# Layer 1's gate product: every second block on two float16 parts, and another order at attention's two ends

## The chip, the cores and the metric

The kernel runs on one NeuronCore of a Trainium2 chip. The metric is device time in microseconds (us), the median of several executions. TensorE (PE) multiplies, VectorE (DVE) and ScalarE (ACT) work on tiles elementwise, GpSimd (POOL) helps with some subtractions, and SyncE (SP) issues most transfers. Each engine takes its instructions strictly in the order in which they were written for it; engines wait for each other through semaphores.

## What is computed

The reference is a two-layer transformer block stack for 256 tokens of width 2048, with 256 context tokens. Layer 0 is a Fourier mixer, layer 1 attention with a sink. The change concerns layer 1:

```python
def _attention_branch(h, hc, w_in, sink, rows, cols, need_ctx):
    q, k, v, z = jnp.split(h @ w_in, [D_BRANCH, D_BRANCH + kvw, D_BRANCH + 2 * kvw], axis=-1)
    ...
    y = jnp.moveaxis(o, 0, 1).reshape(b, n, D_BRANCH) * jax.nn.silu(z)
```

Here `h` is 256 x 2048, `q` and `z` are 256 x 4096 each, and `y` is multiplied by the output weights afterwards (`x + gate * (y @ w_out[1])`). `z` is the gate product of the title.

## The kernel before

Every large product is made of three matmuls on parts (`mm3`: high x high, high x low, low x high), so that two short parts stand for one float32 number. The parts come in two kinds. `half_split` makes two float32r parts of half a loaded weight tile: a copy on ACT (`split`, L66) and a subtraction on DVE (L67). `split16` makes two float16 parts: the tile times a scale on ACT (L137) and the rest on DVE (L138). float16 needs the scale, since its range is small; the scale is a power of two from the sum of squares of the weights.

Layer 1 begins with the keys and values of all 512 tokens, on float16 parts of the activations (`hz`, 16 tiles) in a pool of their own. The activations `hx1` (16 tiles, float32r parts) then serve the queries and the gate.

Then comes the attention loop. The weights are taken in *units*, each half of a 1 MB tile `raw` (three buffers): a q unit has 12 matmuls of 512 columns, a z unit 24 matmuls of 256 columns, an o unit (first output columns) 12 of 512. `units()` writes their order out: q of head 0, and then per group of four blocks the 8 q units of the next head and the 2 x 4 z units of the four blocks of 128 channels; 14 o units at the end. `prep` makes the parts of a unit one unit ahead; their pool `ws` has six buffers, two to a unit.

The blocks b = 0..31 (one pair of heads each) are laid between the units. `stage_s(b)` computes scores on PE (L1500), their maximum on DVE (L1503, tile `mx`), the exponential on ACT (L1507, tile `p`; L1509, `es`), and the probabilities in two float16 parts (`f`; ACT L1522, DVE L1523), which a transposing transfer on SP's queue turns into `ft`. `stage_o(b - 1)` (L1534) multiplies them with the values. The loop body is in this order:

```python
                        pts[b] = stage_s(b)
                filler(4 if b < 32 else 3)
                if b:
                    ...
                        stage_o(b - 1, ft)
```

`filler(n)` emits n units, so a block stands with four units. Ahead of the loop 10 units are emitted (`first = 10`). After the eighth q unit of a head `finish_q` takes the sums of squares (ACT L1365), rotates the queries (`roped`: DVE L1132, L1137, L1138), makes a scale of them (DVE L1371 to L1374, tile `sq`) and puts off the float16 parts `fq` (`q_parts`, ACT L1382, DVE L1383). For head 0 these parts are transposed on PE (`pe_turn`, L1392) and copied back (L1393), and so are the four `f` tiles of the last block, which are the last thing that the loop waits for. A scheduler sets each engine's final order from the order of emission and its own estimate of the durations; it is fixed in the program.

After the loop the remaining output columns are computed on float16 parts: `split16` of `wo1b` tiles (ACT L137, DVE L138) and of `y1` (`y_half`, L1312, L1313).

Of the kernel before, what the change touches and what calls it, by code (L numbers as in the profile page):

```python
# [17 lines left out]
P = 128  # L18
D = 2048
# [13 lines left out]
def tile_dit(ctx: ExitStack, tc: tile.TileContext, a: dict, out: bass.AP):  # L33
# [1106 lines left out]
    with tc.tile_pool(name="h1", reuse_waits="tile", bufs=16) as h1p:  # L1140
        hx1 = []
        v01, vs = [], []
        dsc = h1p.tile([P, 8], F32, name="dsc", bufs=1)
        ksc = h1p.tile([P, 6], F32, name="ksc", bufs=1)
# [4 lines left out]
        with tc.tile_pool(name="kvp", reuse_waits="tile", bufs=2) as kvp:  # L1149
            hz, ends = [], []  # L1150
            oner = kvp.tile([P, P], F32R, name="oner", bufs=1)
            S.activation(oner, ident, AF.Identity, bias=1.0, scale=0.0)
            ropek = act()[:, 0:N].rearrange("p (a b c) -> p a b c", a=2, b=2)
            for k in range(KT):
                z2 = kvp.tile([P, 1024], F16, tag="hz", name="hz", bufs=16)
                t = kvp.tile([P, 512], F32, tag="ht", name="ht")
                for s in range(2):
                    q = slice(s * N, (s + 1) * N)
                    h, l = (z2[:, s * 512 + c : s * 512 + c + N] for c in (0, N))
                    V.scalar_tensor_tensor(t[:, q], x1[k][:, q], gsz[:, k, s : s + 1], r_bc1[:, q] if k else r_ps[s], op0=ALU.mult, op1=ALU.mult)  # L1160
                    with tc.issue_after(a_end) if (k, s) == (0, 1) else nullcontext():
                        a_ = S.activation(h, t[:, q], AF.Identity, bias=shz[:, k, s : s + 1]).ins
                    with tc.issue_after(e) if (k, s) == (0, 1) else nullcontext():
                        e = V.scalar_tensor_tensor(l, t[:, q], shz[:, k, s : s + 1], h, op0=ALU.add, op1=ALU.subtract).ins
                    if s == 0:
                        a_end = a_
                ends.append((a_, e))
                if k == 0:
                    [S.copy(r_bc1[:, i * N : (i + 1) * N], r_ps[i]) for i in range(2)]
                    with tc.issue_after(bc_end), tc.issue_after(a_end):  # L1170
                        x1_turn(0, 3)
                        x1_turn(1, 3)
                hz.append(z2)
# [26 lines left out]
            for kg in range(8):  # L1200
# [16 lines left out]
                for j in range(2):  # L1217
                    k = kg * 2 + j
                    wh, wl = w[j]
                    for tb in range(4):  # L1220
                        c = tb // 2 * 512 + tb % 2 * P
                        for kv in range(2):
                            q = slice(kv * 512, (kv + 1) * 512)
                            mm3(o[tb][kv], hz[k][:, c : c + P], hz[k][:, N + c : N + c + P], wh[:, q], wl[:, q], k == 0, k == KT - 1)
            kr = []
# [33 lines left out]
            for tb in range(4):  # L1259
# [6 lines left out]
                v01.append(va)  # L1266

        y1 = []
        raw1, fin = [None], []
        oA, kg1, yh = [], [0], []  # L1270
        with tc.tile_pool(name="at", reuse_waits="tile", bufs=2) as at:
# [55 lines left out]
            def o1_step(k, os_, wh, wl):  # L1327
# [4 lines left out]
                return r  # L1332
            slot = [0]

# [25 lines left out]
            def finish_q(hk, oq):  # L1360
                sq = at.tile([P, 2, 4], F32, tag="sq", name="sq")
                qr = []
                for tb in range(2):
                    t = act()
                    S.activation(act(), oq[tb], AF.Square, accum_out=sq[:, tb, 0:1])  # L1365
# [5 lines left out]
                V.tensor_scalar(x, sq[:, :, 0], 2.0**-70, None, op0=ALU.max)  # L1371
                V.tensor_scalar(x.bitcast(I32), x.bitcast(I32), 24, 23, op0=ALU.logical_shift_right, op1=ALU.logical_shift_left)
                V.tensor_scalar(up.bitcast(I32), x.bitcast(I32), -1.0, 204.0 * 2**23, op0=ALU.mult, op1=ALU.add)
# [15 lines left out]
            def pe_turn(ft, f, tb):  # L1389
                o = pp.tile([P, 8, P], F16, tag="ps", name="ps")  # L1390
                for j in range(8):
                    PE.transpose(o[:, j, :], f[:, j * P : (j + 1) * P], ident16)  # L1392
                (S.copy if tb == 0 else V.tensor_copy)(ft[:, :, tb, :], o)  # L1393

# [21 lines left out]
            pos = [0]  # L1416

            def prep(u):
                kind, n, i, _ = u
                if kind == "o":  # L1420
                    return w1_next()
                src = (kind, n, i // 2)
                if src not in raws1:
                    raws1[src] = raw(a["wq"][n, i // 2] if kind == "q" else a["wz1"][n])
                return half_split(raws1[src], i % 2)

# [3 lines left out]
            def emit_unit():  # L1430
                if pos[0] >= len(ulist):
                    return
                u = ulist[pos[0]]
                if pos[0] not in ready:
                    ready[pos[0]] = prep(u)
# [25 lines left out]
                else:  # L1461
                    if i == 0:
                        o.append(psum())
                    for k in range(i * 8, i * 8 + 8):
                        q = slice((k % 8) * P, (k % 8 + 1) * P)
                        pe_last[0] = mm3(o[0][:, 0:N], wh[:, q], wl[:, q], hx1[k][:, 0:N], hx1[k][:, N : 2 * N], k == 0, k == KT - 1)
                    if i == 1:
                        th = at.tile([P, N], F32, tag="th", name="th", bufs=3)
                        zs = o[0][:, 0:N]
                        S.activation(th, zs, AF.Tanh, scale=0.5)  # L1470
                        V.scalar_tensor_tensor(th, th, 1.0, zs, op0=ALU.add, op1=ALU.mult)
                        szs[n] = th
                        emit_y(n)

            ydone = set()

            def emit_y(blk):
# [3 lines left out]
                if blk % 2 == 0:  # L1481
                    y1.append(act())
                V.scalar_tensor_tensor(y1[blk // 2][:, (blk % 2) * N : (blk % 2 + 1) * N], obs[blk, 1], dsc[:, blk // 4 : blk // 4 + 1], szs.pop(blk), op0=ALU.mult, op1=ALU.mult)
                if blk % 2:
# [52 lines left out]

            first = 10
            for i in range(first):
# [20 lines left out]
            for b in range(33):  # L1560
# [20 lines left out]
        with tc.tile_pool(name="fin", reuse_waits="tile", bufs=1) as fp:  # L1581
# [243 lines left out]
```

## Time and profile before

| | us |
|---|---|
| time before, median of 3 runs | 1749.79 (1749.52 to 1751.82) |
| the profiled execution's own time | 1751.69 |
| its span, first to last instruction | 1749.9 |
| PE busy | 1708.5 (98%) |
| DVE busy | 1376.4 (79%) |
| ACT busy | 1103.4 (63%) |
| keys and values begin, attention loop begins and ends (us from the span's start) | about 1003, 1124, 1611 |

Matmuls are pipelined, so "busy" of PE is not a measure of its load; the distance between the starts of two matmuls is what one costs. DVE and ACT rows have a duration some 0.1 us longer than the distance between two starts.

### The profile page before, as it was taken

Reading aid. Unit: us, or ns where it says so; the run is one execution under the profiler, and the core shown is the slowest. Engines: PE = TensorE matmul, PEld = TensorE weight load, DVE = VectorE, ACT = ScalarE, POOL = GpSimd, SP = SyncE. Lnnn points to the kernel's source line nnn. Section 1 sums busy time; section 2 is a strip of 40 time slices with the busy share of each in tenths; the row PEclk is TensorE's granted clock in tenths of the full one; section 3 lists DMA queues with packets and bytes.
Section 4 is the critical chain, followed back from the end, with each engine's and each line's share of the span. In section 5 each row is a group of like instructions: output and inputs, shape, how many; then the busy total and the mean of one; then the engine's idle time right before and its main releaser. Section 6 shows DMA issues by size and latency. Waiting matters only on the chain. (4 is left out here: it accounts for less than half of the span.)

```text
span 1749.9 us, 28309 instructions
## 1 busy us (share of the span) xinstructions
PE 1708.5 (98%) x10379; PEld 1131.3 (65%) x10379; DVE 1376.4 (79%) x2390; ACT 1103.4 (63%) x2111; POOL 281.2 (16%) x429
## 2 busy tenths in 40 slices
PE   6999999999999999999999999999999999998997
PEld 4679999644444444446444745688788888975464
DVE  5779888798776787778689585888899888985755
ACT  5545555477777755455335497677777778775643
POOL 0002111211222104202310210200000000050001
PEclk9999999999999999999999999999999999999999
DMA  9998998878998969976997595489999999986643
GB/s 394 417 357 254 275 269 258 304 267 310 342 306 307 314 238 349 388 269 228 393 358 247 147 370 187 138 238 220 235 230 233 218 246 221 233 217 238 236 169 120
DMA packets 249195, 469.94 MB, mean 269 GB/s; under 512 B 171392, under 2 KB 171792, under 8 KB 222176
## 3 DMA queue, kind: packets, MB, share of 16 engines
q1 hardware_dynamic: 197568, 335.60, 59.0%
q0 software_dynamic: 47344, 125.58, 22.6%
q10 hardware_dynamic: 4144, 6.95, 1.2%
q8 instruction: 81, 1.33, 0.3%
q14 instruction: 58, 0.48, 0.1%
HBM read 419.30 MB, written 12.59 MB: 247 GB/s over the span
## 5 line engine op out<-in xcount | busy, mean ns | idle before, releaser
L67 DVE TENSOR_TENSOR wl<-raw,wh 128x1024 fp32r<-128x1024 f32 x152 | 189.7, 1262 | 50.1 <-ACT wh L66 41.9
L146 PE MATMUL ps<-act,wf 128*128 128x512 f16 x512 | 194.0, 379 | 0.0
L147 PE MATMUL ps<-act,wf 128*128 128x512 f16 x512 | 191.1, 379 | 0.0
L145 PE MATMUL ps<-act,wf 128*128 128x512 f16 x512 | 189.8, 379 | 1.1 <-ACT act L877 0.4
L66 ACT CAST wh<-raw 128x1024 fp32r<-128x1024 f32 x152 | 156.9, 1045 | 46.9 <-PE ps L146 29.9
L145 PE MATMUL ps<-y,wf 128*128 128x512 f16 x448 | 169.8, 379 | 0.8 <-ACT wf L137 0.8
L146 PE MATMUL ps<-y,wf 128*128 128x512 f16 x448 | 169.8, 379 | 0.0
L145 PEld LDWEIGHTS <-wf 128*128 128x128 f16 x960 | 93.8, 98 | 114.0 <-ACT wf L137 4.7
L147 PEld LDWEIGHTS <-wf 128*128 128x128 f16 x960 | 93.9, 98 | 113.1
L147 PE MATMUL ps<-y,wf 128*128 128x512 f16 x448 | 164.9, 379 | 0.0
L146 PEld LDWEIGHTS <-wf 128*128 128x128 f16 x960 | 93.9, 98 | 109.0
L137 ACT ACTIVATE wf<-raw,nrm 128x1024 f16<-128x1024 f32 x56 | 63.5, 1145 | 132.6 <-PE ps L147 73.7
L145 PE MATMUL ps<-h,wh 128*128 128x256 f32 x512 | 144.3, 282 | 0.0
L147 PE MATMUL ps<-h,wl 128*128 128x256 f32 x512 | 142.6, 279 | 0.1
L146 PE MATMUL ps<-h,wh 128*128 128x256 f32 x512 | 142.7, 279 | 0.0
L1507 ACT ACTIVATE p<-ps,mx 128x512 f32<-128x512 f32 x128 | 87.8, 686 | 86.4 <-DVE mx L1503 86.1
L138 DVE SCALAR_TENSOR_TENSOR wf<-raw,tn,wf 128x1024 f16<-128x1024 f32 x64 | 79.8, 1281 | 42.6 <-ACT wf L137 42.6
L829 ACT ACTIVATE act<-act 128x512 f32<-128x512 f32 x178 | 109.4, 616 | 5.2 <-DMA act<-in_wo 4.6
L146 PE MATMUL ps<-wl,h 128*128 128x512 f32 x256 | 101.6, 397 | 0.0
L147 PE MATMUL ps<-wh,h 128*128 128x512 f32 x256 | 101.2, 395 | 0.0
L145 PEld LDWEIGHTS ps<-h,wh 128*128 128x128 f32 x512 | 96.1, 188 | 7.1 <-issue 5.9
L145 PE MATMUL ps<-wh,h 128*128 128x512 f32 x256 | 100.4, 403 | 0.0
(430 smaller groups left out, 4656.4 us busy)
## 6 DMA issues: line engine op xcount, KB each, us to landing
raw<-in_wz SPq DMA_DIRECT2D x64, 1024.0 KB, 5.5
raw<-in_awp SPq DMA_DIRECT2D x32, 1024.0 KB, 12.8
zr<-in_adw SPq DMA_DIRECT2D x64, 512.0 KB, 6.9
wa<-in_adw POOLq DMA_DIRECT2D x64, 512.0 KB, 6.7
act<-in_wo POOLq DMA_DIRECT2D x128, 256.0 KB, 7.4
raw<-in_wo SPq DMA_DIRECT2D x32, 1024.0 KB, 8.4
raw<-in_wq SPq DMA_DIRECT2D x32, 1024.0 KB, 5.3
raw<-in_wu SPq DMA_DIRECT2D x32, 1016.0 KB, 7.2
```

Source lines behind the costliest of these rows:

```text
L66: last_cast[0] = S.copy(h, src).ins
L67: last_sub[0] = eng.tensor_tensor(l, src, h.bitcast(F32), op=ALU.subtract).ins
L137: last_cast[0] = S.activation(w[:, 0], src, AF.Copy, scale=up).ins
L138: last_sub[0] = V.scalar_tensor_tensor(w[:, 1], src, up, w[:, 0], op0=ALU.mult, op1=ALU.subtract).ins
L145: PE.matmul(o, wh, xh, start=start, stop=False)
L146: PE.matmul(o, wh, xl, start=False, stop=False)
L147: return PE.matmul(o, wl, xh, start=False, stop=stop).ins
L829: S.activation(t, t, AF.Square, accum_out=c)
L1507: S.activation(pt[hh, tb], so[hh, tb], AF.Exp, bias=mx[:, hh, tb : tb + 1], scale=-1.0, accum_out=sm[:, hh, tb : tb + 1])
```

## The change

Of the 32 gate blocks the 16 odd ones (`zset`) are multiplied on float16 parts: stationary are the weights, moving are the x halves of `hz`, which therefore stay alive through the loop, in eight tiles of the pool `act` (`zx`). Such a block needs a scale of its weights. It is taken from the loaded tile itself (`z_scale`): a square with its sum on ACT over the whole 128x2048 tile, a matmul with ones that sums over the partitions, and three operations on one column on DVE. `z_ahead` loads the tile four units ahead of its block and computes the scale two units ahead. The scale is taken back in the tanh's scale and, by one more column operation (`y_factor`), in the product with the attention's output.

At the attention's beginning 11 units instead of 10 stand ahead of the loop, and `finish_q` takes both sums of squares first and computes the scale between the two rotations. At its end one unit stands ahead of the transposes of the last block and one behind them, and the copies of these transposes no longer follow the next weights. Each tile is loaded as before, though an odd block's now ahead of that of the even block before it (SP's order z1, z0, z3, z2 in a group); the rest of the arithmetic is the same.

```diff
-                z2 = kvp.tile([P, 1024], F16, tag="hz", name="hz", bufs=16)
+                if k % 2 == 0:
+                    zx.append(actp.tile([P, 1024], F16, tag="act", name="hzx"))
+                z2 = zx[k // 2][:, k % 2 * 512 : k % 2 * 512 + 512], kvp.tile([P, 512], F16, tag="hz", name="hz", bufs=16)
...
+        zset = range(1, NB, 2)
+        ekh = h1p.tile([P, 1], F32, name="ekh", bufs=1)
+        V.tensor_scalar(ekh.bitcast(I32), ek.bitcast(I32), -(2.0**23), None, op0=ALU.add)
...
             def finish_q(hk, oq):
                 sq = at.tile([P, 2, 4], F32, tag="sq", name="sq")
-                qr = []
                 for tb in range(2):
-                    t = act()
                     S.activation(act(), oq[tb], AF.Square, accum_out=sq[:, tb, 0:1])
-                    roped(t, oq[tb], tb, actp, "act")
-                    qr.append(t)
-                if hk:
-                    prep_kk(hk)
                 x, up, sc = (sq[:, :, c] for c in (1, 2, 3))
+                qr = [act(), act()]
+                roped(qr[0], oq[0], 0, actp, "act")
                 V.tensor_scalar(x, sq[:, :, 0], 2.0**-70, None, op0=ALU.max)
                 V.tensor_scalar(x.bitcast(I32), x.bitcast(I32), 24, 23, op0=ALU.logical_shift_right, op1=ALU.logical_shift_left)
                 V.tensor_scalar(up.bitcast(I32), x.bitcast(I32), -1.0, 204.0 * 2**23, op0=ALU.mult, op1=ALU.add)
+                roped(qr[1], oq[1], 1, actp, "act")
                 V.tensor_scalar(sc.bitcast(I32), x.bitcast(I32), kx.bitcast(I32), -30.0 * 2**23 - 2.0**31, op0=ALU.add, op1=ALU.add)
+                if hk:
+                    prep_kk(hk)
...
+            def z_scale(n):
+                c = at.tile([P, 4], F32, tag="zc", name="zc", bufs=4)
+                S.activation(zjunk, raws1["z", n, 0], AF.Square, accum_out=c[:, 0:1])
+                o = psum()[:, 0:1]
+                PE.matmul(o, ones.broadcast_to([P, P]), c[:, 0:1], start=True, stop=True)
+                x, zup[n], zdn[n] = (c[:, j : j + 1] for j in (1, 2, 3))
+                V.tensor_scalar(x.bitcast(I32), o.bitcast(I32), 24, 23, op0=ALU.logical_shift_right, op1=ALU.logical_shift_left)
+                V.tensor_scalar(zup[n].bitcast(I32), x.bitcast(I32), -1.0, 204.0 * 2**23, op0=ALU.mult, op1=ALU.add)
+                V.tensor_scalar(zdn[n].bitcast(I32), x.bitcast(I32), ekh.bitcast(I32), 2.0**23, op0=ALU.add, op1=ALU.max)
+
+            def z_ahead(c):
+                for d in (4, 2):
+                    if c + d < len(ulist):
+                        u = ulist[c + d]
+                        if u[0] == "z" and u[1] in zset and u[2] == 0:
+                            if d == 4:
+                                w_load(u)
+                            else:
+                                z_scale(u[1])
...
-                return half_split(raws1[src], i % 2)
+                t = w_load(u)
+                return split16(t, i, zup[n]) if kind == "z" and n in zset else half_split(t, i % 2)
...
+                z_ahead(pos[0])
...
-                        pe_last[0] = mm3(o[0][:, 0:N], wh[:, q], wl[:, q], hx1[k][:, 0:N], hx1[k][:, N : 2 * N], k == 0, k == KT - 1)
+                        t = hz[k][0] if n in zset else hx1[k]
+                        pe_last[0] = mm3(o[0][:, 0:N], wh[:, q], wl[:, q], t[:, 0:N], t[:, N : 2 * N], k == 0, k == KT - 1)
...
+            def y_factor(blk):
+                d = dsc[:, blk // 4 : blk // 4 + 1]
+                if blk in zset:
+                    V.tensor_scalar(zdn[blk], zdn[blk], d, 2.0, op0=ALU.mult, op1=ALU.mult)
+                    d = zdn[blk]
+                return d
...
-            first = 10
+            first = 11
...
-                filler(4 if b < 32 else 3)
+                filler(4 if b < 32 else 1)
                 if b:
                     ft, fs = pts.pop(b - 1)
+                    if fs:
+                        with tc.issue_after(pe_last[0]):
+                            for (hh, tb), f in fs.items():
+                                turned[tb] = pe_turn(ft[hh], f, tb)
+                        filler(1)
                     with tc.issue_after(pe_last[0]):
-                        for (hh, tb), f in fs.items():
-                            pe_turn(ft[hh], f, tb)
                         stage_o(b - 1, ft)
...
-                with tc.issue_after(f_last[0]), tc.issue_after(f_last[1]):
+                with tc.issue_after((turned if kg else f_last)[0]), tc.issue_after((turned if kg else f_last)[1]):
```

The scheduler then places the new work among the old. Three places show how.

First ACT, in a block of the loop in which a head's queries end (its second block in a group of four; the same rows stand in six of the eight groups). `p` and `es` are the exponentials, `act,sq` the squares of the queries, `wh` float32r weights, `wf` float16 ones, `zjunk,zc` the new square. Before:

```order
L1507 ACTIVATE p,sm<-ps,mx 128x512
L1509 ACTIVATE es<-mx,sink 128x2
L66 CAST wh<-raw 128x1024
L1522 ACTIVATE f<-p,sm 128x512 x4
L1365 ACTIVATE act,sq<-ps 128x512
L66 CAST wh<-raw 128x1024
L1365 ACTIVATE act,sq<-ps 128x512
```

And now:

```order
L1548 ACTIVATE p,sm<-ps,mx 128x512
L1550 ACTIVATE es<-mx,sink 128x2
L1434 ACTIVATE zjunk,zc<-raw 128x2048
L1369 ACTIVATE act,sq<-ps 128x512 x2
L137 ACTIVATE wf<-raw,zc 128x1024 x2
L1563 ACTIVATE f<-p,sm 128x512 x4
```

The new square (of the group's second odd block) stands behind the exponentials and ahead of the squares of the queries; behind these come the float16 weights of the group's first odd block.

Then DVE in the same block, from the reciprocal of the sums on. Before:

```order
L1511 RECIPROCAL sm<-sm 128x4
L67 TENSOR_TENSOR wl<-raw,wh 128x1024
L1523 SCALAR_TENSOR_TENSOR f<-p,sm,f 128x512 x4
L1132 TENSOR_TENSOR act<-ps,rope 128x512
L1137 TENSOR_TENSOR rt<-ps,rope 128x16x16 x2
L67 TENSOR_TENSOR wl<-raw,wh 128x1024
```

And now:

```order
L1552 RECIPROCAL sm<-sm 128x4
L1132 TENSOR_TENSOR act<-ps,rope 128x512
L1137 TENSOR_TENSOR rt<-ps,rope 128x16x16 x2
L1373 TENSOR_SCALAR sq<-sq 128x2
L1132 TENSOR_TENSOR act<-ps,rope 128x512
L1137 TENSOR_TENSOR rt<-ps,rope 128x16x16 x2
L1138 TENSOR_TENSOR act<-act,rt 128x512
L1374 TENSOR_SCALAR sq<-sq 128x2
L138 SCALAR_TENSOR_TENSOR wf<-raw,zc,wf 128x1024 x2
L1138 TENSOR_TENSOR act<-act,rt 128x512
```

The low parts `wf` of the first odd block stand behind the rotation of the queries, which itself reads what the two squares of ACT left.

Last ACT at the end of attention, behind the parts of the last block (`f`); `ft` are the copies of the transposes on PE that the last `stage_o` needs. Before:

```order
L1522 ACTIVATE f<-p,sm 128x512 x4
L1312 ACTIVATE yf<-act,adab 128x512 x3
L66 CAST wh<-raw 128x1024 x3
L137 ACTIVATE wf<-raw,adab 128x1024 x2
L1312 ACTIVATE yf<-act,adab 128x512
L137 ACTIVATE wf<-raw,adab 128x1024 x2
L1312 ACTIVATE yf<-act,adab 128x512
L1393 COPY ft<-ps 128x8x128 x2
```

And now:

```order
L1563 ACTIVATE f<-p,sm 128x512 x4
L1318 ACTIVATE yf<-act,adab 128x512 x3
L66 CAST wh<-raw 128x1024 x3
L137 ACTIVATE wf<-raw,adab 128x1024 x2
L1318 ACTIVATE yf<-act,adab 128x512
L1398 COPY ft<-ps 128x8x128 x2
L137 ACTIVATE wf<-raw,adab 128x1024 x2
```

The copies moved ahead of the second pair of output weights.

More of the change, by code (lines that the diff above doesn't have):

```diff
@@ L1142, in tile_dit @@
         v01, vs = [], []
+        hz, zx = [], []
         dsc = h1p.tile([P, 8], F32, name="dsc", bufs=1)
@@ L1149, in tile_dit @@
         with tc.tile_pool(name="kvp", reuse_waits="tile", bufs=2) as kvp:
-            hz, ends = [], []
+            ends = []
             oner = kvp.tile([P, P], F32R, name="oner", bufs=1)
@@ L1158, in tile_dit @@
                     q = slice(s * N, (s + 1) * N)
-                    h, l = (z2[:, s * 512 + c : s * 512 + c + N] for c in (0, N))
+                    h, l = (z2[s][:, c : c + N] for c in (0, N))
                     V.scalar_tensor_tensor(t[:, q], x1[k][:, q], gsz[:, k, s : s + 1], r_bc1[:, q] if k else r_ps[s], op0=ALU.mult, op1=ALU.mult)
@@ L1391, in pe_turn @@
                 for j in range(8):
-                    PE.transpose(o[:, j, :], f[:, j * P : (j + 1) * P], ident16)
-                (S.copy if tb == 0 else V.tensor_copy)(ft[:, :, tb, :], o)
+                    pe_last[0] = PE.transpose(o[:, j, :], f[:, j * P : (j + 1) * P], ident16).ins
+                return (S.copy if tb == 0 else V.tensor_copy)(ft[:, :, tb, :], o).ins
             def units():
@@ L1416, in tile_dit, with w_load @@
             pos = [0]
+            def w_load(u):
+                kind, n, i, _ = u
+                src = (kind, n, i // 2)
+                if src not in raws1:
+                    raws1[src] = raw(a["wq"][n, i // 2] if kind == "q" else a["wz1"][n])
+                return raws1[src]
+            zup, zdn, zjunk = {}, {}, at.tile([P, D], BF16, name="zjunk", bufs=1)
+            def z_scale(n):
[16 more added lines that the diff above has]
+                                z_scale(u[1])
             def prep(u):
@@ L1469, in emit_unit @@
                         zs = o[0][:, 0:N]
-                        S.activation(th, zs, AF.Tanh, scale=0.5)
+                        S.activation(th, zs, AF.Tanh, scale=zdn[n] if n in zset else 0.5)
                         V.scalar_tensor_tensor(th, th, 1.0, zs, op0=ALU.add, op1=ALU.mult)
```

11 lines of the change are left out of this document (4 added, 7 removed).

## Prediction

> **What bounds the kernel now.** I read the page's busy shares first, then windows by stage, PE's waits, the timelines at attention's two ends, and last one block of the loop on each engine.
>
> ```profile
> PE 1708.5 (98%) x10379; PEld 1131.3 (65%) x10379; DVE 1376.4 (79%) x2390; ACT 1103.4 (63%) x2111; POOL 281.2 (16%) x429
> ```
>
> PE is busy 98% of the span, so on the whole only a cheaper matmul or a removed wait gains. Two windows of layer 1, the loop's body and a stretch behind it with two short waits; columns are busy time and count by engine (PE, PEld, DVE, ACT, POOL), then granted clock, DMA share, GB/s.
>
> ```profile
> 1139.00:1538.00 399.00, 398.92 (x3099) 335.35 (x3100) 355.26 (x660) 307.64 (x613) 19.17 (x12) 1.00 0.94 231
> 1545.00:1560.00 15.00, 13.16 (x78) 8.81 (x77) 12.16 (x16) 14.25 (x34) 15.00 (x16) 1.00 0.71 201
> ```
>
> In the body PE never rests, DVE is at 89% and ACT at 77%. The holes are at the two ends of the loop; PE's longest waits between 1100 and 1615 us name them (total, times, longest):
>
> ```profile
> PE ps L1534 <- ACT ft L1393: 6.9, 1, 6.9
> PE ps L1392 <- ACT fq L1382: 3.4, 1, 3.4
> PE ps L146 <- DVE wl L67: 1.8, 2, 0.9
> ```
>
> So there is something to win at the ends, and something to lose in the body, where PE waits for nothing today.
>
> **Term 1, the matmuls of the odd blocks.** A gate matmul has 256 columns. Its distance on float32r parts, first and last of 33 starts, and beside it the float16 matmuls of the keys and values at 512 columns, first and last of 25 starts:
>
> ```profile
> 1205.03 0.28 PE L145 MATMUL ps<-h,wh 128*128 128x256 f32 x1
> ...
> 1208.80 0.28 PE L147 MATMUL ps<-h,wl 128*128 128x256 f32 x1
> ...
> 1079.68 0.38 PE L145 MATMUL ps<-wf,hz 128*128 128x512 f16 x1
> ...
> 1084.87 0.38 PE L145 MATMUL ps<-wf,hz 128*128 128x512 f16 x1
> L1246 PE MATMUL ps<-ksc,ones x8: 164/210/250, 1085.7 to 1096.3; 128*128 128x1 f32 x8
> ```
>
> 3.77/32 = 117.8 ns, and 5.19/24 = 216.3 ns, half of it 108.1. Sixteen blocks of 48 matmuls make 768 x 9.7 ns = -7.4 us. Float16 at 256 columns does not stand in the trace: 117.8 (nothing gained) is one bound, 108.1 the other; I take 108.1, because at 512 columns the distance is also the column count's. Each odd block adds a one-column matmul of the kind of L1246, 16 x 0.21 = +3.4. Term 1 is -4.0, between -4.0 and +3.4.
>
> **Term 2, the loop's beginning.** ACT and PE around head 0's queries, and for comparison PE in a later block:
>
> ```profile
> 1120.88 1.33 ACT L1382 ACTIVATE fq<-act,sq 128x512 f16<-128x512 f32 x2 [1.81 <-DVE sq L1373]
> 1116.66 0.40 PE L145 MATMUL ps<-wh,h 128*128 128x512 f32 x1
> ...
> 1117.83 0.39 PE L147 MATMUL ps<-wh,h 128*128 128x512 f32 x1
> 1121.66 2.07 PE L1392 MATMUL ps<-ident,fq 128*128 128x128 f16 x16 [3.44 <-ACT fq L1382]
> 1124.41 1.04 PE L1500 MATMUL ps<-kkh,qt 64*128 64x512 f16 x4 [0.68 <-ACT qt L1393]
> 1127.09 0.80 PE L145 MATMUL ps<-wh,h 128*128 128x512 f32 x1
> 1309.98 0.60 PE L1500 MATMUL ps<-kkh,qt 64*128 64x512 f16 x4
> 1311.38 0.50 PE L145 MATMUL ps<-wh,h 128*128 128x512 f32 x1
> 1324.25 0.61 PE L1500 MATMUL ps<-kkh,qt 64*128 64x512 f16 x4
> 1121.60:1131.00 9.40, 8.66 (x43) 0.64 0.17 70
> 1601.60:1608.00 6.40, 6.39 (x20) 0.64 0.51 182
> ```
>
> PE waits 3.44 for the scale and 0.68 for `qt`, and behind that the clock is 0.64 for 9.4 us: the scores take 2.68 where a later block's take 1.40, the transposes about 1.0 too much, the first matmuls 0.5; 2.8 together. The eleventh unit is not new work; it moves from the loop to here, and its 12 matmuls of 0.234 (five starts from 1116.66 to 1117.83), 2.8 us, fill the hole. The scale also no longer waits for the second rotation. I leave 1.4 of the 4.1 idle and no half clock: 2.7 + 2.8 = -5.5. Bounds: -7 (nothing left) and -2.7 (the clock still drops).
>
> **Term 3, the loop's end.**
>
> ```profile
> 1597.86 2.19 ACT L137 ACTIVATE wf<-raw,adab 128x1024 f16<-128x1024 f32 x2 [5.16 <-DMA raw<-in_wo1b]
> 1600.57 1.90 ACT L1393 COPY ft<-ps 128x1024 f16<-128x1024 f16 x2
> 1592.74 1.96 PE L1392 MATMUL ps<-ident,f 128*128 128x128 f16 x32
> 1601.61 0.37 PE L1534 MATMUL ps<-ft,v 128*64 128x256 f16 x1 [6.90 <-ACT ft L1393]
> ```
>
> ACT's copies of 1.9 us stand behind weights whose tile lands at 1597.86, and PE waits 6.90 for them. With the copies ahead of these weights and a unit of 2.8 us between transposes and their use, the copies are covered; 6.4 us of clock 0.64 cost another 6.4 x 0.36 = 2.3. I leave 0.5: -8.7. The next to be late is the same tile's weights, at 1597.86 + 2.2 = 1600.1; from 1594.7 PE has the last product (a block's 14.27 less 1.4 of scores and four units of 2.8: 1.6), a unit (2.8) and the first pair's 24 matmuls of 0.216 (5.2) in hand, 9.6 us to 1604.3, so it does not reach them. Bounds -9.2 and 0, if it does.
>
> **Term 4, the loop's body: the new chain.** By sums no engine becomes the bound; the rows are of the same operations elsewhere in the kernel:
>
> ```profile
> L251 ACT ACTIVATE dump<-xn x4: 1906/1910/1911, 6.5 to 15.3; 128x2048 f32<-128x2048 f32 x4
> L138 DVE SCALAR_TENSOR_TENSOR wf<-raw,tn,wf 128x1024 f16<-128x1024 f32 x64 | 79.8, 1281 | 42.6 <-ACT wf L137 42.6
> ...
> L67 DVE TENSOR_TENSOR wl<-raw,wh 128x1024 fp32r<-128x1024 f32 x112 | 136.1, 1230 | 25.4 <-ACT wh L66 24.9 <-PE ps L146 0.3
> ```
>
> A square of a whole tile, 1.91 with 0.2 for the sum's reading (L1365's, below), is 2.1 us of ACT, so 16 of them bring ACT from 308 to about 341 of 399; four operations on one column, by L1371's 0.16 (below), and slightly longer low parts (1281 against some 1230 ns) bring DVE from 355 to about 367, 92%. What matters is the order. The diffed rows show the float16 weights of a group's first odd block, in the block where a head's queries end, behind exponentials, a square (of the second odd block) and the queries' squares on ACT, and behind the rotation on DVE. Here is that block before, scores at 1309.98:
>
> ```profile
> 1311.68 0.81 DVE L1503 CUSTOM_DVE_ANT_0 ps<-ps,mask,nsink 128x512 f32<-128x512 f32 x1
> 1315.95 0.17 DVE L1510 SCALAR_TENSOR_TENSOR sm<-sm,es 128x4 f32<-128x4 f32 x1 [1.21 <-ACT es L1509]
> 1319.22 0.58 ACT L1365 ACTIVATE act<-ps 128x512 f32<-128x512 f32 x1
> 1319.70 0.20 ACT L1365 ACTIVATION_READ_ACCUMULATOR act<-ps 128x1 f32 x1
> 1319.79 1.05 ACT L66 CAST wh<-raw 128x1024 fp32r<-128x1024 f32 x1
> 1318.03 2.73 DVE L1523 SCALAR_TENSOR_TENSOR f<-p,sm,f 128x512 f16<-128x512 f32 x4
> 1323.08 0.69 DVE L1132 TENSOR_TENSOR act<-ps,rope 128x512 f32<-128x512 f32 x1
> 1324.34 0.16 DVE L1371 TENSOR_SCALAR sq<-sq 128x2 f32<-128x2 f32 x1
> 1324.41 0.69 DVE L1138 TENSOR_TENSOR act<-act,rt 128x512 f32<-128x512 f32 x1
> 1313.66 4.81 SPq L50 DMA_DIRECT2D raw<-in_wz  x2
> raw<-in_wz SPq DMA_DIRECT2D x64, 1024.0 KB, 5.5
> ```
>
> Counted from the scores: the exponentials end at 5.9 (the sums that wait for them start at 1315.95). The new square takes it to 8.0, the first square of the queries (0.7) to 8.7. Only then does DVE rotate: 1.26 (1323.08 to 1324.34) twice, one L1138 of 0.6 and two column operations of 0.07, 3.3 together, to 12.0; the low half (1.28) ends at 13.2. PE has, from the same zero, scores 1.4, a queries' unit 2.8, the one-column matmul 0.2 and two float32r gate units of 24 x 0.1178 = 2.8 each: it asks at 10.1, its third matmul, the first with low weights, at 10.3. So PE waits 2.9 where it waited for nothing. `wl` of float32r did not stand behind the rotation; that is the step that turns the change around.
>
> More of the same kind: in the block before, the first odd block's own square stands ahead of the fourth exponential; DVE has 1.21 us of slack there against 2.1, so it enters this block about 0.8 late. Behind the low halves (14.4) DVE still has an L1138, four `f` (2.7), two `wl` and a `th` to do, some 6.2 us, to 20.6, while the next scores, a block's 14.3 later (1309.98 to 1324.25) and 3.7 late, begin at 18.0: their maxima start 2.6 in, not 1.7, and the second odd block's low half comes 0.2 to 1.6 late there; I take 0.9. In the group's first block the last queries' weights lose 0 to 0.6; 0.3. That is 4.9 a group. The tile may land late as well: its load was issued 3.7 after the scores, and 5.5 later is 9.2, which is 3.3 after the exponentials; the change issues it some units earlier, so I take 0. A group thus costs 2.9 to 9.1. Seven groups have a head's queries in them (head 0's stand ahead of the loop): 7 x 4.9 = +34.3, between +20 and +64.
>
> The other edits are near nothing: keeping half of `hz` in the pool `act` costs nothing as long as the queue of `act` users is unchanged; I found no wait of PE for it, and its bounds are 0 and half a microsecond. The loads' order on SP, odd tile first, lies inside the spans above. The copies and `y_factor` are counted in DVE's.
>
> **Sum** against the profiled execution: 1751.7 - 4.0 - 5.5 - 8.7 + 34.3 = 1767.8. That execution lies 1.9 above the median of the runs shown, 1749.8; on the median's scale the forecast is 1766, about 0.9% slower. Its own range takes stalls of 3.5 to 8 us a group: 1756 to 1788.
>
> **Rivals.** First, the other side: the weights come in time. The break-even is 18.2 us of gains over seven groups, 2.6 us each, and my surest part of the stall, 2.9, is barely above it. If ACT's exponentials run earlier than in the old block, because the loads of float32r copies ahead of them shrink (an odd block needs no `wh` there), the chain starts up to a copy's 1.05 us earlier per block, and each group's stall falls below 2. Between no stall, 1749.8 - 18.2 = 1731.6, and 2.2 a group, 1747: faster. Against it: PE's scores, not ACT's backlog, release the maxima at 1311.68. Chance 0.26.
>
> Second, the stalls take the clock with them. The wait of 3.44 us up to 1121.66 was followed by a stretch at 0.64 that cost 9.4 x 0.36 = 3.4, the wait of 6.90 by one that cost 2.3; two of 0.9 left it at 1.00. Stalls of 3.5 us a group that each did this would add 7 x 2.3 to 7 x 3.4, 16 to 24: 1782 to 1790. The taken stall of 3.7 lies at the edge. Chance 0.16. The Trainium skill ("TensorE: Matmul & The Clock Gate", Part 1, the HAM clock gate) says that the array falls to half rate after an idle window of about 3.4 us, and that this window runs freely. By that rule a wait of 3.7 would only rarely contain a whole window, so few of the seven would pay, about 1766 to 1772; the trace agrees that 3.44 can be enough and that 0.9 is not.
>
> Third, the change doesn't do what it says: float16 at 256 columns is no faster (+7.4), or the end's wait turns into one for the tile (+8.7), both above the forecast, 1773 to 1775 each. Chance 0.06 for results that these alone would put beyond the range; I count them into the forecast's range.
>
> **How the numbers follow.** The forecast (some stall of 3.5 us or more a group, full clock) has 0.50, the first rival 0.26, the clock 0.16, the third 0.06, and 0.02 is for what I don't see. A measurement of this kernel can tell about 0.2%, 3.5 us, from no change: 1746.3 to 1753.3. Between the rival's upper end and the forecast's lower end little lies there: same 0.06, faster 0.25, slower 0.69. The range leaves out the lower half of the faster case (0.13) and the top of the clock's (0.07): 1738 to 1790.
>
> **What would show it.** In the changed kernel: `hz` gate matmuls 108 ns apart; in seven groups a wait of PE for `wf` from L138 of 3 to 4 us, and a second of about 1; a block of 18 in place of 14.3 there; DVE at 92% or so; no hole above 1.5 us at the loop's beginning and 1 at its end, with the clock at 1.00 in both. I am wrong if PE's wait for L138 is below 2.6 us a group, which would mean that the exponentials or the rotation end earlier than the row of before puts them, or if the hole at the end stays.

## The result, and the profile after

The changed kernel takes 1797.31 us (1792.81 to 1798.1) against 1749.65 before: ratio 1.0265, 95% interval 1.0246 to 1.0283. Slower was right; 1766 was not, and 1797 lies outside the range. The profiled execution took 1798.1, its span is 1796.3, 46.4 more than before. The page's shares of busy time barely moved; PE went from 98% to 96%:

```profile
PE 1720.6 (96%) x10411; PEld 1122.0 (62%) x10411; DVE 1383.3 (77%) x2455; ACT 1139.1 (63%) x2143; POOL 277.3 (15%) x429
```

The windows at the loop's beginning and in its body (columns as in the prediction):

```profile
1121.00:1131.00 10.00, 9.07 (x52) 6.21 (x52) 6.22 (x14) 9.14 (x17) 0.00 (x0) 1.00 0.50 189
1139.00:1560.00 421.00, 383.31 (x2830) 302.04 (x2829) 333.60 (x669) 317.75 (x598) 13.96 (x12) 0.96 0.81 202
```

The beginning has lost its hole, and its clock, 0.64 before, is 1.00. The body, in which PE was busy without a break, now has 38 us of idle and a clock of 0.96. PE's waits between 1131 and 1560 us, and below them the two rows of ACT's waits that come from the new scale:

```profile
PE ps L147 <- DVE wf L138: 18.4, 8, 2.6
PE ps L145 <- ACT wf L137: 16.0, 8, 3.5
PE ps L146 <- DVE wl L67: 2.3, 5, 0.5
PE ps L145 <- ACT wh L66: 0.9, 2, 0.6
...
ACT zjunk L1434 <- DMA raw<-in_wz: 26.7, 14, 4.9
...
ACT wf L137 <- DVE zc L1439: 2.6, 6, 0.8
```

PE waits 34.4 us for float16 weights, all but 1.2 of it in the seven blocks that the prediction named, those in which a head's queries end. ACT in turn stands in front of the new square 26.7 us, because the tile has not landed; for the finished scale it stands 2.6. One such block, scores at 1331.82:

```profile
1331.82 0.61 PE L1541 MATMUL ps<-kkh,qt 64*128 64x512 f16 x4
...
1338.12 0.29 ACT L1550 ACTIVATE es<-mx,sink 128x2 f32<-128x2 f32 x1
1340.02 1.91 ACT L1434 ACTIVATE zjunk<-raw 128x2048 bf16<-128x2048 f32 x1 [1.61 <-DMA raw<-in_wz]
1341.93 0.58 ACT L1369 ACTIVATE act<-ps 128x512 f32<-128x512 f32 x1
1343.07 2.18 ACT L137 ACTIVATE wf<-raw,zc 128x1024 f16<-128x1024 f32 x2
...
1342.63 0.69 DVE L1132 TENSOR_TENSOR act<-ps,rope 128x512 f32<-128x512 f32 x1 [3.76 <-ACT act L1369]
1345.90 2.48 DVE L138 SCALAR_TENSOR_TENSOR wf<-raw,zc,wf 128x1024 f16<-128x1024 f32 x2
...
1344.27 0.28 PE L145 MATMUL ps<-hzx,wf 128*128 128x256 f16 x1 [2.12 <-ACT wf L137]
1344.39 0.27 PE L146 MATMUL ps<-hzx,wf 128*128 128x256 f16 x1
1347.24 0.40 PE L147 MATMUL ps<-hzx,wf 128*128 128x256 f16 x1 [2.58 <-DVE wf L138]
...
1349.78 0.42 PE L147 MATMUL ps<-hzx,wf 128*128 128x256 f16 x1
...
1351.70 0.42 PE L147 MATMUL ps<-hzx,wf 128*128 128x256 f16 x1
...
1342.48:1345.90 3.42, 0.39 (x2) 1.00 0.00 0
1345.90:1352.72 6.82, 5.48 (x30) 0.50 0.43 156
1352.72:1356.13 3.41, 3.41 (x41) 1.00 1.12 195
```

Read it downwards: exponentials to 6.6 us behind the scores, 1.61 of standing for the tile, the square to 10.1, a square of the queries, the rotation of 3.3, the first low half, and PE goes on at 15.4. Without a wait it would have come to the low half at 10.4. PE stands 2.12 and 2.58 with two matmuls between, and the matmuls behind that are 213 ns apart instead of 110: the clock has fallen to 0.50 (the last three rows: window, PE's busy time and count, clock, DMA). The block takes 22.0 us where it took 14.3.

At the end the copies are ahead of the weights whose tile was late, as the diff has it, and two new waits stand in the place of the old one:

```profile
1637.78 1.50 PE L1575 MATMUL ps<-ft,v 128*64 128x256 f16 x23 [1.89 <-DMA ft<-f]
1650.12 0.27 PE L1575 MATMUL ps<-ft,v 128*64 128x256 f16 x1 [2.28 <-ACT ft L1398]
...
1642.65 1.99 ACT L66 CAST wh<-raw 128x1024 fp32r<-128x1024 f32 x2 [5.67 <-DMA raw<-in_wo1a]
1646.37 2.19 ACT L137 ACTIVATE wf<-raw,adab 128x1024 f16<-128x1024 f32 x2 [1.73 <-DMA raw<-in_wo1b]
1649.08 1.90 ACT L1398 COPY ft<-ps 128x1024 f16<-128x1024 f16 x2
```

The copies now stand behind two other tiles, of which the first lands 5.67 us after ACT was ready for it.

### The profile page after: what moved, and what is told of

Read it like the earlier page. It is cut to its first block, busy times and chain, and to the rows that moved or that the text cites. A ratio compares the mean times of both kernels' runs of the same rounds, so it can differ in the third digit from the quotient of the medians.

```text
span 1796.3 us, 28446 instructions
## 1 busy us (share of the span) xinstructions
PE 1720.6 (96%) x10411; PEld 1122.0 (62%) x10411; DVE 1383.3 (77%) x2455; ACT 1139.1 (63%) x2143; POOL 277.3 (15%) x429
## 5 line engine op out<-in xcount | busy, mean ns | idle before, releaser
L145 PEld LDWEIGHTS <-wf 128*128 128x128 f16 x1216 | 120.8, 99 | 142.3 <-ACT wf L137 21.9
L147 PEld LDWEIGHTS <-wf 128*128 128x128 f16 x1216 | 121.2, 100 | 138.9 <-DVE wf L138 20.6
L146 PEld LDWEIGHTS <-wf 128*128 128x128 f16 x1216 | 121.2, 100 | 113.9
L67 DVE TENSOR_TENSOR wl<-raw,wh 128x1024 fp32r<-128x1024 f32 x120 | 150.4, 1271 | 36.3 <-ACT wh L66 25.6
L66 ACT CAST wh<-raw 128x1024 fp32r<-128x1024 f32 x120 | 122.3, 1042 | 49.9 <-PE ps L146 23.8
L138 DVE SCALAR_TENSOR_TENSOR wf<-raw,tn,wf 128x1024 f16<-128x1024 f32 x64 | 79.8, 1281 | 42.2 <-ACT wf L137 41.5
L1544 DVE CUSTOM_DVE_ANT_0 ps<-ps,mask,nsink 128x512 f32<-128x512 f32 x128 | 97.2, 814 | 1.5 <-PE ps L1541 1.5
L1564 DVE SCALAR_TENSOR_TENSOR f<-p,sm,f 128x512 f16<-128x512 f32 x128 | 90.1, 762 | 5.9 <-ACT f L1563 5.9
L147 PE MATMUL ps<-hzx,wf 128*128 128x256 f16 x256 | 76.7, 300 | 18.4 <-DVE wf L138 18.4
L145 PE MATMUL ps<-hzx,wf 128*128 128x256 f16 x256 | 76.4, 298 | 16.0 <-ACT wf L137 16.0
```

Of the source, the lines that this page charges most:

```text
L66: last_cast[0] = S.copy(h, src).ins
L67: last_sub[0] = eng.tensor_tensor(l, src, h.bitcast(F32), op=ALU.subtract).ins
L138: last_sub[0] = V.scalar_tensor_tensor(w[:, 1], src, up, w[:, 0], op0=ALU.mult, op1=ALU.subtract).ins
L145: PE.matmul(o, wh, xh, start=start, stop=False)
L146: PE.matmul(o, wh, xl, start=False, stop=False)
L147: return PE.matmul(o, wl, xh, start=False, stop=stop).ins
```

## The experiments

Eleven kernels ran, all from the changed kernel. Times are medians, ratios are to the kernel before.

**The ends alone.**

```diff
-        zset = range(1, NB, 2)
+        zset = ()
```

> All 32 gate blocks on float32r again, the changed order at attention's two ends kept. If the whole loss lies in the loop's float16 blocks, as the waits of the changed kernel say, this is before less the ends' gain: 5.8 us at the beginning (measured up to the second block's scores) and 3 to 9 at the end: 1735 to 1741 us. Rival, that the ends (the eleventh unit, the queries' order) disturb the loop themselves: 1750 or above.

1737.65 us, ratio 0.9924 (0.9909 to 0.9938): faster than both kernels, and within what was expected. The body is whole, and both ends gain (windows of the beginning and the body):

```profile
1121.00:1131.00 10.00, 9.07 (x55) 6.23 (x55) 8.24 (x17) 9.36 (x18) 0.00 (x0) 1.00 0.48 193
1139.00:1538.00 399.00, 399.00 (x3120) 336.60 (x3119) 355.28 (x662) 310.62 (x620) 19.85 (x16) 1.00 0.93 231
```

The span is 14.8 shorter. The second block's scores stand at 1136.3 instead of 1139.0 with a unit of 2.8 us more done, so the beginning gives 5.5 and the rest 9.3. The float16 blocks therefore cost 59.7 us by themselves (1797.3 less 1737.7).

**One scale for all blocks.** The scale comes from the first odd tile; the other 15 squares, their sums and column operations are left out, so the kernel holds only for weights whose tiles are alike. (`y_factor` writes to a tile of its own, since all blocks share the scale.)

```diff
             def z_scale(n):
+                if n != 1:
+                    zup[n], zdn[n] = zup[1], zdn[1]
+                    return
```

> Sixteen float16 blocks as in the change, tiles loaded ahead as in the change, but the scale is computed from the first odd tile only and used for all, so 15 of the squares, one-column matmuls and column operations are gone. Theory (the stall is the chain of tile's landing, square, queries' squares, rotation, low parts): without the first two links the low half is ready about 11.3 us after the scores against 10.1 asked, a wait of 1 to 1.6 us in seven blocks, clock at 1.00: 1737 to 1750 us. Rival (float16 parts come late whatever the scale, behind the rotation, or DVE is short of time): the waits stay near 5 us and the time above 1780.

1750.29, ratio 0.9998 (0.9988 to 1.0007), at the upper end of what the theory gave. The waits for `wf` are gone but for one; PE's waits between 1131 and 1560 us:

```profile
PE ps L1579 <- DMA ft<-f: 7.0, 10, 1.0
PE ps L147 <- DVE wf L138: 1.1, 1, 1.1
```

So it is the scale that costs 47 of the 60 us, not float16 parts as such. The rest, 12.6 and the 5.9 that the matmuls should bring, is hardly in the weights any more. In the profiled executions 6.8 us more than with the ends alone lie between the scores of the second and of the thirtieth block, where PE waits for transposed probabilities, and 5.6 behind them; the part behind was not followed up.

**The scale's work with nobody reading it.** As the last kernel, but the other tiles are squared all the same.

```diff
                 if n != 1:
+                    S.activation(zjunk, raws1["z", n, 0], AF.Square, accum_out=c[:, 0:1])
                     zup[n], zdn[n] = zup[1], zdn[1]
                     return
```

> As e2_onescale (one scale for all, from the first odd tile), but each other odd tile is squared and summed on ACT all the same, and nobody reads the result. e2 took 1750.3, the change 1797.3. Theory A (the weights wait for their own scale: the chain of data): without that dependence the squares cost little, 1750 to 1758. Theory B (what counts is that ACT, which takes its work strictly in order, stands before a tile that has not landed and then squares for 2.1 us, while the exponentials behind it wait): 1775 to 1797.

1788.41, ratio 1.022 (1.0199 to 1.024). Thirty-eight of the 47 us come back although no weight waits for a result. Its waits of PE and of ACT:

```profile
PE ps L145 <- ACT wf L137: 24.2, 7, 4.2
PE ps L147 <- DVE wf L138: 8.5, 7, 2.0
...
ACT zjunk L1435 <- DMA raw<-in_wz: 37.3, 14, 4.1
```

The time is that of theory B: ACT, in order, stands before a tile on its way and then squares it, while the exponentials, the queries' squares and the parts behind it are ready to run, and this alone can cost 38 us. It is not quite the change's own loss: without a reader the scheduler put the square ahead of three exponentials in five of the seven blocks, where the change has it behind all four in six, so ACT stands longer (37.3 instead of 26.7 us). Theory A has little left in the change, where ACT waits 2.6 us in all for the scale's result.

**Shorter squares.**

```diff
-                S.activation(zjunk, raws1["z", n, 0], AF.Square, accum_out=c[:, 0:1])
+                S.activation(zjunk[:, 0:128], raws1["z", n, 0][:, 0:128], AF.Square, scale=4.0, accum_out=c[:, 0:1])
```

The scale is here that of a sixteenth of the tile.

> The changed kernel, but each square reads only the first 128 of the tile's 2048 columns (and multiplies by 16 through its scale, so the scale of the weights stays about the same): 0.3 us of ACT in place of 2.1, the wait for the tile's landing stays. Order on PE and SP as in the change. Theory (landing and square stand one behind the other on ACT, ahead of exponentials, queries' squares and float16 weights): 1.7 us less in each of two blocks a group, and some of the clock's loss, 7 x 2.5 to 7 x 5: 1762 to 1780 us. If the landing alone sets the time and the square hides: 1797.

1780.39, ratio 1.0166 (1.0149 to 1.0183): 16.9 less than the change, at the edge of what was expected.

```profile
PE ps L147 <- DVE wf L138: 18.4, 8, 2.6
PE ps L145 <- ACT wf L137: 10.8, 5, 2.9
...
ACT zjunk L1434 <- DMA raw<-in_wz: 40.1, 15, 5.7
```

The wait for landing grew from 26.7 to 40.1 us: ACT arrives earlier and stands longer, also because the scheduler put the shorter square ahead of two exponentials in six of the seven blocks. The 1.7 us that a square is shorter only partly reach PE, and with the other order the run does not give the square's price alone.

**Tiles from another queue.**

```diff
-                    raws1[src] = raw(a["wq"][n, i // 2] if kind == "q" else a["wz1"][n])
+                    raws1[src] = raw(a["wq"][n, i // 2] if kind == "q" else a["wz1"][n], nc.gpsimd if kind == "z" and n in zset else None)
```

> The odd blocks' tiles are loaded from GpSimd's queue, where they stand behind no transposing transfers; all else as in the change. Theory (the square waits for its tile, 26.7 us in 14 waits, because the load is issued behind the four transposes of the block before): the square's waits vanish, each stall shrinks by about 1.6 us and with it part of the clock's loss: 7 x 1.6 to 7 x 5 less, 1762 to 1786 us. Rival (the tile is not what the square is late for, or the buffer comes free no earlier): 1797, no change.

1810.04, ratio 1.0323 (1.03 to 1.0347): slower, outside every expectation. ACT's wait, one of the loads on GpSimd's queue, ahead of a block with scores at 1322.5, and the square of its tile; last the same square of the changed kernel, where the block's scores stand at 1316.8:

```profile
ACT zjunk L1434 <- DMA raw<-in_wz: 37.5, 13, 6.8
...
1320.56 0.56 POOL L50 DMA_DIRECT2D raw<-in_wz  x1 [7.59 <-DVE wl L67]
1327.48 1.91 ACT L1434 ACTIVATE zjunk<-raw 128x2048 bf16<-128x2048 f32 x1 [2.18 <-DMA raw<-in_wz]
...
1322.75 1.91 ACT L1434 ACTIVATE zjunk<-raw 128x2048 bf16<-128x2048 f32 x1 [1.53 <-DMA raw<-in_wz]
```

The queue was free for 7.59 us and the load waited for a buffer: `raw` has three, and one comes free when DVE has the low parts of the tile three loads ago. The tile still landed a little earlier, 5.0 us behind the scores instead of 6.0; over thirteen blocks with such a square the median gain is 0.9. But the scheduler had put the square ahead of three of the four exponentials, in the change of one, so ACT came to it 1.7 us earlier and stood longer. That the transposing transfers hold the load back, my first theory, is not what sets it in this run; how much of the change's waits they make, a run with this other order does not say.

**The tile of the block before.** The square reads a tile that was expected to be there already, so the scale is the neighbour's.

```diff
-                S.activation(zjunk, raws1["z", n, 0], AF.Square, accum_out=c[:, 0:1])
+                S.activation(zjunk, raws1["z", n - 1, 0], AF.Square, accum_out=c[:, 0:1])
```

> The changed kernel, but the square reads the tile of the even block before, which has landed long ago, so ACT never stands before a tile that is on its way; the square itself stays, and the weights wait for its result. The scheduler now puts the probabilities (four f, 2.6 us) ahead of the float16 weights on ACT and DVE in the queries' block. Theory B: no wait for landing and a square in ACT's slack, but parts behind f: a stall near 4 us in seven blocks with some loss of clock, no loss in the others: 1770 to 1785. If the landing costs nothing: 1797 or above.

1789.91, ratio 1.0229 (1.0214 to 1.0244): above the range that I gave. ACT still waited 14.3 us in 10 places for a tile, and the scheduler's new order put the four `f` ahead of the float16 weights:

```profile
PE ps L145 <- ACT wf L137: 27.8, 8, 5.2
PE ps L147 <- DVE wf L138: 7.6, 9, 0.9
```

Two things changed at once, so this run does not say what the landing is worth. In this order, with the weights behind `f`, PE stands for them 35.4 us, as much as in the change (34.4).

**Half of the blocks.** Only the second odd block of each group, then only the first:

```diff
-        zset = range(1, NB, 2)
+        zset = range(3, NB, 4)
```

> The change with only the second odd block of each group (3 of 4) on float16, each with its own scale and its tile loaded ahead. Its weights are due one block after the queries' end. Theory (the stall needs the float16 weights in the block of the queries' end, and a square in front of them): nearly no stall: the ends' 1737.7 less 3.7 for the matmuls, 1.7 for the small ones, and 0 to 2 us a group for a square that waits: 1736 to 1750. Rival (each float16 block costs alike): half of 60, 1768.

> The change with only the first odd block of each group (1 of 4) on float16. Its weights are due in the block of the queries' end, but no square stands ahead of them there. Theory: the low half is ready some 11.7 us after the scores against 10.3: 1.4 a group and about 0.8 for the square in the block before, with the clock at 1.00: 1737.7 - 2 + 7 x 2.2, 1747 to 1758 us; the two halves (this and e7_mod3) then add up to far less than the 60 us of both together. Rival (each float16 block costs alike): 1768.

1777.76, ratio 1.0152 (1.0137 to 1.0167), and with `range(1, NB, 4)` 1781.17, ratio 1.0151 (1.0106 to 1.0196). My theory that the loss needs both blocks together fell, and so did the rival that each block costs alike: each half alone costs 40.1 and 43.5 of the 60, not 30. PE's waits with the second odd blocks only:

```profile
PE ps L147 <- DVE wl L67: 8.5, 10, 1.2
PE ps L145 <- ACT wh L66: 7.8, 7, 2.0
PE ps L147 <- DVE wf L138: 5.8, 7, 0.9
PE ps L145 <- ACT wf L137: 3.0, 4, 1.5
```

Here no float16 weight is due in the queries' block, and PE waits in it for float32r weights instead, `wh` and `wl`, about 2.2 us: the square stands ahead of three exponentials, and what ACT does behind them is late whatever it is. It fits theory B, from which I had not yet argued. The first odd blocks alone left 22 us of waits in the body and 12.3 in two waits at the loop's end; their runs lay from 1765 to 1783, so that number is loose.

**Work for PE in the wait.** Eight matmuls whose result is overwritten, ahead of the first odd block's first matmul; the rows of ACT and SP are the change's, word for word.

```diff
+                        if n in zset and n % 4 == 1 and n < 28:
+                            for _ in range(8):
+                                PE.matmul(o[0], hz[0][0][:, 0:P], hz[0][0], start=True, stop=True)
```

> The changed kernel with 8 useless float16 matmuls of 512 columns (1.7 us) ahead of the first odd block's first matmul in each of the first seven groups, where PE waits 2.1 and then 2.6 us; their results are overwritten. The order of the work on ACT, DVE and SP is unchanged. Theory (after 4.7 us of almost unbroken idle the clock is at 0.61 to 0.82 for some 10 us, which costs 2 to 3 us a group): with 2.6 us of idle at most the clock stays at 1.00 and the kernel gets faster by 14 to 20 us though it does more work: 1777 to 1783 us. Rival (the clock is not set by this idle time): 1797 if the matmuls hide in the wait, up to 1809 if not.

1791.13, ratio 1.0233 (1.0218 to 1.0249): 6.2 us less with 12 us more of work, less than half of what I expected. The waits for `wf` on ACT fell from 16.0 to 4.6 us; those on DVE stayed (18.0). The clock over the body rose from 0.96 to 0.98, and its stretches at half clock sum to 20.5 us instead of 37.6. Two groups of this run, each with one wait for the low half, of 2.36 us up to 1412.04 and of 2.58 up to 1475.08:

```profile
1412.04 0.28 PE L147 MATMUL ps<-hzx,wf 128*128 128x256 f16 x1 [2.36 <-DVE wf L138]
...
1409.44:1412.85 3.41, 1.05 (x11) 1.00 0.01 2
1412.85:1416.26 3.41, 3.41 (x19) 0.50 0.56 175
...
1470.88:1474.29 3.41, 1.61 (x8) 1.00 0.01 2
1474.29:1477.71 3.42, 2.63 (x24) 1.00 0.12 22
```

The wait of 2.36 us halved the clock from 1412.85 to 1416.26, the longer one did not touch it. So idle time costs clock here, as the second rival said, and the eight matmuls saved only a part of it. What tells the two apart is where the wait lies. All 133 changes of the clock in the thirteen traces stand, within a run, whole multiples of 3.413 us apart. In stretches cut at these points, and by the profile's busy time of PE, whose matmul ends are modelled, the clock fell after each stretch at full clock in which PE was busy for 45% or less, after none with more than 52%, and in between after some; it came back after a stretch of some 80% or more and stayed at half after less. The first wait lies inside one stretch and leaves PE 31% of it; the second is divided between two, with 47% and 77%.

**Loads in the old place.** One scale as above, and the odd tiles loaded as before, one unit ahead (but the first); then the same with all 32 blocks on float16.

```diff
                             if d == 4:
-                                w_load(u)
+                                if u[1] == 1:
+                                    w_load(u)
```

> As e2_onescale (one scale, from the first odd tile, for all sixteen float16 blocks), and the tiles are loaded in the old place and order, one unit ahead, but for the first. Theory (in e2 the loads issued ahead wait for a buffer at the head of SP's queue and hold back the transposing transfers, which PE then waits for): the float16 blocks cost nothing any more and bring their 7.4 us: the ends alone gave 1737.7, so 1728 to 1735 us. Rival (float16 parts are dearer for DVE and ACT than float32r ones): 1737 or above.

> As e5_noahead, with all 32 gate blocks on float16 parts and the one scale from tile 0. If float16 parts with a scale that is known early are free, another 768 matmuls of 9.7 ns less: 1721 to 1728 us. If DVE, 2% busier for longer low parts, becomes late: above e5_noahead.

1746.84, ratio 0.998 (0.9967 to 0.9993), and 1749.42, ratio 0.9987 (0.9978 to 0.9997). Both missed: the 5.9 us (twice that) of cheaper matmuls do not arrive. PE's first row of waits in the body, of the one and of the other:

```profile
PE ps L1580 <- DMA ft<-f: 4.9, 7, 1.1
...
PE ps L1580 <- DMA ft<-f: 14.5, 11, 2.9
```

In the second kernel part of the loss lies ahead of the body: its second block's scores stand at 1144.3, those of the first kernel at 1135.8. With the scale known early, the scheduler's order has float16 weights ahead of the probabilities `f` on ACT in the queries' block, and the transposes of `f` come late. That this order is the cause was read from it, not tested: a version with `f` first was not run.

## Why the prediction was right or wrong

The terms, in us, as predicted and as the traces have them:

| term | predicted | measured |
|---|---|---|
| 1, matmuls | -4.0 | -3.8 |
| 2, beginning | -5.5 | -5.8 |
| 3, end | -8.7 | -2.7 (-9.3 without the float16 blocks) |
| 4, PE's idle in the body | +34.3 | +37.6 |
| clock in the body | 0 | about +16 |

*Term 1* was right in the sum; its two parts were off by 1.4 and 1.2 us and balance. Float16 matmuls of the changed kernel at full clock:

```profile
1355.19 0.28 PE L145 MATMUL ps<-hzx,wf 128*128 128x256 f16 x1
...
1357.72 0.27 PE L147 MATMUL ps<-hzx,wf 128*128 128x256 f16 x1
...
1336.12 0.28 PE L1436 MATMUL ps<-zc,ones 128*128 128x1 f32 x2
1336.26 0.36 PE L145 MATMUL ps<-h,wh 128*128 128x256 f32 x1
```

They are 2.53/23 = 110 ns apart (108.1 taken), 768 x 7.8 = 6.0 us; a one-column product takes 0.14 (0.21 taken), 2.2 for sixteen.

*Term 2* was right: the second block's scores are 3.0 earlier with a unit of 2.8 more done, and the clock is 1.00. The rotation and the scale in another order did what the sum said.

*Term 3* failed in the changed kernel at one sentence, "it does not reach them": I looked only at the tile that was late before. Between the scores of the thirtieth block (1537.9 before, 1589.8 after) and the span's end lie 212.0 and 206.5 us; 2.8 of that is the unit, 2.7 is left. Behind the disturbed loop other tiles land late, and the copies stand behind those. With the loop undisturbed the term holds (9.3). Why these tiles were late was not tried.

*Term 4*: the total of the idle was close, 16.0 + 18.4 + 2.3 + 0.9 = 37.6, and the place was the one named, but of the releasers only the low parts: that PE would also stand for the high parts from ACT, 1.4 to 3.5 us in each of the seven blocks, is not in the sum. PE's wait for L138 alone was 2.0 to 2.6 there, at the border of what I had called being wrong, not because the exponentials or the rotation ended earlier but because PE had already stood. The tile's landing, which I took as 0 because "the change issues it some units earlier", took 1.6 in this block; the run with the other queue showed a load that waits for a buffer, which an earlier issue does not help. In its place the second odd block, for which I had 0.9, cost nothing in six of seven groups. That the errors balanced is luck. I had also told the stall as one of the rotation and of data; the unread squares show that ACT's standing, without the data, can cost most of it.

*The clock* is the step that made the number wrong: the sum has it at 0 in the body. I had its price, 16 to 24 us, and put it into a rival with a chance of 0.16, since "the taken stall of 3.7 lies at the edge". The trace has seven stretches at half clock, one in each group: 6.83 us from 1151.34, 1216.19, 1281.04 and 1345.90, 3.41 from 1410.75, 1475.60 and 1540.46. Of these 37.6 us PE is idle for 5.0; half of the rest, about 16, is lost. No single wait of the body reached the 3.44 us that I had as the measure but one, and all seven groups paid. The length of one wait was the wrong measure: what counts is how little PE works in a stretch of 3.41, and two waits with two matmuls between leave it 0.39 us (1342.48 to 1345.90 above). The Trainium skill's rule ("TensorE: Matmul & The Clock Gate", Part 1, the HAM clock gate) is that the rate halves after an idle window of about 3.4 us, and by it I expected few of the seven to pay. The traces agree with the length of the window, 3.413 us, but not with my reading that nothing may run in it: in the run with the eight matmuls, 1.05 us of work in one window did not keep the clock up.

With 16 for the clock, 6.0 less at the end and 3.3 more idle, 1767.8 becomes 1793; the profiled execution took 1798.1. Most of the 5 us between lies in how a wait is counted. Its row begins at the end of the last matmul, but the next could have started before that end: 1344.39 to 1347.24 is 2.85, the wait 2.58, and 0.11 is the usual distance, so the wait cost 2.74. That is 0.16 more for each of 23 waits, 3.7 in all.

The first rival, weights in time, was wrong: 4.1 to 5.4 us of stall a group against a break-even of 2.6. The third was half right: the end's wait did turn into one for tiles.

## What to carry to other kernels

An instruction that waits for a transfer stops everything behind it on its engine: before new work is put into a full engine's order, ask what stands behind it, and whether a buffer, not the issue, sets when its data lands. Price the stalls of PE with the half clock that may follow: not by the longest wait, but by how much PE still works in a stretch of 3.4 us. Measure parts of a bundle apart: here the ends gain 0.8% and the float16 blocks lose more than four times that.

## What was not expected of the hardware

The clock changed only at points 3.413 us apart, and a stretch between two of them did not have to be empty to halve it: PE busy for up to 45% was too little in every case, 1.05 us of 3.41 among them. So a single wait of 2.36 us, behind unbroken work, cost clock, and one of 2.58 in the same execution, which lay across such a point, did not. The two waits of 0.9 us before the change left it at 1.00.

Useless matmuls made the kernel 6.2 us faster.
